# Score matmuls of even and odd heads by turns, value products one unit later, attention branch by rows first

## The chip, the core and the metric

The kernel runs on one NeuronCore of a Trainium2 chip. TensorE (PE in the rows) multiplies, ScalarE (ACT) and VectorE (DVE) do the elementwise work, GpSimd (POOL) a few powers, SyncE (SP) starts the DMAs. The metric is the time of one execution in microseconds of the device (us), less is better. Three runs of the kernel before gave 952.95, 954.09 and 954.66 us, median 954.09 us.

## What is computed

Two transformer blocks over one sequence of 256 tokens and 1024 features, float32. The first has a short convolution, a spatial gate, a mixture of 32 experts and a gated projection. The second, in which the change lies, is this, cut to what matters:

```
h = rmsnorm(x, norm_mix_pre)
conv_in, q, k, v, g_conv, g_att = split(h @ w_in)
u = silu(layernorm(causal_depthwise_conv(glu(conv_in), 31 taps)))
conv_out = u @ w_conv_branch + b_conv_branch
# stick-breaking attention, 8 heads of 64, queries in blocks of 128
z = einsum('bqhd,bkhd->bhqk', q, k) / 8
log_1m = where(s < t, log_sigmoid(-z), 0)
a = where(s < t, exp(log_sigmoid(z) + (reverse cumsum(log_1m) - log_1m)), 0)
att = einsum('bhqk,bkhd->bqhd', a, v)
att_out = att @ w_att_branch
merged = sigmoid(g_conv) * conv_out + sigmoid(g_att) * att_out
x = x + rmsnorm(merged @ w_out, norm_mix_post)
x = x + feed-forward(x)
```

## The kernel before

All 256 tokens are worked on at once, as two blocks `t` of 128. Weights stream from HBM in chunks of 1 MB, each cut into units of 128x1024 numbers. A unit is split by ACT (`whi`, L174 or L179) and DVE (`wlo`, L175 or L180) into a coarse and a fine part, and PE multiplies with both (`features`, L412; `tokens`, L423): 12 matmuls of 128x512 or 24 of 128x256 for a unit. Up to eight units are split ahead of the one in use; a split buffer comes free when PE is through with the unit that held it. After the experts four raw buffers of 1 MB hold the chunks in flight.

The order on every engine is the order in which the code is written; no scheduler changes it. `unit()` takes the next unit. In that call it lets the stream split ahead and run what was deferred (`ws.defer`), then does some taps of the depthwise convolution on DVE, and then the steps that the tables `ATT_AT`, `SIGMOIDS_AT` and `LN_AT` put at that unit's number. Only after that are the unit's own matmuls written. Units 4 to 15 give q, k and half of the convolution's input, 16 to 31 the two gates (four `n` of four units), 32 to 35 the attention branch.

The eight heads go in two groups `g`, four heads each, two even and two odd. A head's 64 features lie in one half of the 128 rows: even heads in rows 0 to 63, odd ones in 64 to 127. The steps of a group are: `att_z` (L1253, the scores, 12 float32 matmuls, each two records in the trace; then L1258, four bf16 matmuls for the mask), `att_exp` (L1263 to L1265), `att_log` (L1270), `att_add` (L1274, L1275), `att_sum` (L1279 to L1281), `att_a` (L1285, L1286) and `att_v` (L1296, L1297, the value products, whose result a deferred ACT copy L402 and a DVE subtraction L403 split into the coarse and fine `att`). The scores of even heads go to PSUM banks 4 and 5, those of odd heads to banks 6 and 7; `att_v` writes to the free halves of banks 5 and 7.

At units 32 to 34 the layer norm of the convolution stands among the branch: `ln_center` (L1365, the means, into bank 4; L1367 and L1368 centre and square; then `bias_parts`, L1342 to L1349), `ln_var` (L1374, sums of squares, into bank 5; L1377, a power on POOL, L1382) and `ln_out` (L1391 to L1397). `a_post` (L1408) multiplies the attention gate with the branch.

Of the kernel before, what the change touches and what calls it, by code (L numbers as in the profile page):

```python
# [46 lines left out]
OUT_AUTO = ()  # L47
CBN = 4
XT_AT = (5, 13)
ATT_AT = ((14, 14, 14, 14, 18, 18, 22), (25, 25, 26, 27, 30, 30, 31))  # L50
SIGMOIDS_AT = (28, 33)
LN_AT = (32, 33, 34)

# [169 lines left out]
def block_kernel(ctx: ExitStack, tc: tile.TileContext, x, pT, pk, rows, brow, wsT, bsp, w_1, w_gate,  # L223
                 w_up, w_down, w_ple_proj, w_2, out, dbg=None):
# [3 lines left out]
    nc = tc.nc  # L228
# [16 lines left out]
    def gain(name, k0):  # L245
        return lambda a: pc(name, k0 + a)

    gm4 = consts.tile([128, 8], F32, name="gm4")
    ws = Stream(nc, [(rawa, RAW_A), (rawb, RAW_B)], partp)
    ring = [RING]  # L250

    def add(src, a, b, cuts, gain=None, late=False, apart=False):
        pool, aside = 0, ASIDES.get(len(ws.chunks))
        if not late and not aside:
            pool = 0 if ring[0] % (RAW_A + RAW_B) < RAW_A else 1
            ring[0] += 1
        return ws.add(src, a, b, cuts, pool, gain, aside, apart)

    halves2 = [(0, 2, 0, 512), (2, 2, 0, 512)]
# [22 lines left out]
    def add_2(n, wide, gain=None):  # L282

        for _ in range(n):
            add(w_2[at_2[0]], 2 if wide else 4, 1024 if wide else 512, full2 if wide else halves2,
                gain and gain(at_2[0]), late=True)
            at_2[0] += 1

    at_2 = [0]
    add_2(4, True, lambda n: gain("g_ple", 2 * n))  # L290
    add_2(22, False)
    add_2(4, True)
    for j in range(13):
        if j < 11:
# [26 lines left out]
    def warm(ps, n):  # L321

        for _ in range(n):
            nc.tensor.matmul(ps[:, 0:128], ident_bf, ones_bf, start=True, stop=True, skip_group_check=True)  # L324
# [46 lines left out]
    def four(ap, n=4):  # L371
        return ap.rearrange("p (i t) -> p i t", i=n)
# [43 lines left out]
    def tokens(ps, hi, lo, u, k0, first, last, ts=(0, 1), cs=None):  # L416

        w = min(u.nb, 512)
        for k in range(u.na):
            for t in ts:  # L420
                for n, (a, b) in enumerate(((hi, u.hi), (hi, u.lo), (lo, u.hi))):
                    for c in cs or range(u.nb // w):
                        nc.tensor.matmul(ps[t][c], a[:, k0 + k, t, :], b[:, k, c * w:(c + 1) * w],  # L423
                                         start=(first and k == 0 and n == 0),
                                         stop=(last and k == u.na - 1 and n == 2), skip_group_check=True)
# [65 lines left out]
    with ExitStack() as pa:  # L491
# [90 lines left out]
        gu, csb, z = four(S3), four(S2), four(S1)  # L582
# [544 lines left out]
    def bank2(i):  # L1127
        return [bank(2 * i), bank(2 * i + 1)]
# [31 lines left out]
    def unit():  # L1160
        u = ws.get()
        conv_some(CONV_N[at_unit[0]] if at_unit[0] < len(CONV_N) else 0)
        for f in steps.get(at_unit[0], ()):
            f()
        at_unit[0] += 1
        return u
# [56 lines left out]
    qT = ab.tile([128, 4, 256], F32, name="qT")  # L1223
    kT = ab.tile([128, 4, 256], F32, name="kT")
# [16 lines left out]
    Z, EZ = {}, {}  # L1241

    def att_z(g):


        Z[g] = [bank2(2 + odd) for odd in range(2)]
        EZ[g] = [ab.tile([128, 768], F32, name=f"ez{odd}", bufs=2) for odd in range(2)]
        warm(Z[g][0][0], 0 if g else WARM4)
        for odd, (z, y) in enumerate(Z[g]):
            r = slice(odd * 64, odd * 64 + 64)  # L1250
            for o, ks, qs in ((z[:, 0:256], 0, 0), (z[:, 256:512], 0, 128), (y[:, 0:256], 128, 128)):
                for i in range(2):
                    nc.tensor.matmul(o[:, 128 * i:128 * i + 128], kT[r, 2 * g + i, ks:ks + 128],  # L1253
                                     qT[r, 2 * g + i, qs:qs + 128], start=(i == 0 and (ks, qs) != (0, 128)),
                                     stop=False, skip_group_check=True)
        for e, (z, y) in zip(EZ[g], Z[g]):
            for o in (z, y):
                nc.tensor.matmul(o[:, 0:256], ident_bf, cap[:, None, :].to_broadcast([128, 2, 128]),  # L1258
                                 start=False, stop=False, skip_group_check=True)
# [46 lines left out]

    for g, at in enumerate(ATT_AT):
        for n, f in zip(at, (att_z, att_exp, att_log, att_add, att_sum, att_a, att_v)):
            steps.setdefault(n, []).append(lambda f=f, g=g: f(g))
# [89 lines left out]
    for n, f in zip(LN_AT, (lambda: (ln_center(), bias_parts()), ln_var, ln_out)):  # L1399
        steps.setdefault(n, []).append(f)  # L1400

    for c in range(2):
        for i in range(2):
            tokens([[pa_[t][c]] for t in range(2)], ahv, alv, unit(), 2 * i, i == 0, i == 1)

        def a_post(c=c):
            for t in range(2):
                nc.vector.tensor_mul(G[t][:, 2 + c, :], G[t][:, 2 + c, :], pa_[t][c])  # L1408

        ws.defer(a_post)  # L1410
# [3 lines left out]
    for t in (1, 0):  # L1414
        for c in range(2):
            for f in range(4):
                nc.tensor.matmul(pc2[t][c][:, f * 128:f * 128 + 128],
                                 sel[:, 4 * c + f:4 * c + f + 1].to_broadcast([72, 128]), b3[2], start=(f == 0),
                                 stop=False, skip_group_check=True)
# [236 lines left out]
```

## Time and profile before

| | before |
|---|---|
| runs, us | 952.95, 954.09, 954.66 (median 954.09) |
| profiled execution, time | 954.75 us |
| profiled execution, span from first to last instruction | 953.1 us |
| mean granted TensorE clock | 0.955 of full speed |
| PE busy | 828.5 us (87%) |
| DVE busy | 395.6 us (42%) |
| ACT busy | 310.5 us (33%) |
| DMA | 288.98 MB, 303 GB/s on average |

The first 560 us hold the first block; there the experts' weights set the pace. From there to the end PE is busy nearly without a break, and ACT and DVE are busy beside it. The change lies between 635 and 730 us. Busy shares of the whole span say little on that stretch: what matters is which engine waits for which, place by place.

### The profile page before, as it was taken

Reading aid. Unit: us, or ns where it says so; the run is one execution under the profiler, and the core shown is the slowest. Engines: PE = TensorE matmul, PEld = TensorE weight load, DVE = VectorE, ACT = ScalarE, POOL = GpSimd, SP = SyncE. Lnnn points to the kernel's source line nnn. Section 1 sums busy time; section 2 is a strip of 40 time slices with the busy share of each in tenths; the row PEclk is TensorE's granted clock in tenths of the full one; section 3 lists DMA queues with packets and bytes.
Section 4 is the critical chain, followed back from the end, with each engine's and each line's share of the span. In section 5 each row is a group of like instructions: output and inputs, shape, how many; then the busy total and the mean of one; then the engine's idle time right before and its main releaser. Section 6 shows DMA issues by size and latency. Waiting matters only on the chain.

```text
span 953.1 us, 12639 instructions
## 1 busy us (share of the span) xinstructions
PE 828.5 (87%) x5187; PEld 543.6 (57%) x5187; DVE 395.6 (42%) x708; ACT 310.5 (33%) x488; POOL 12.8 (1%) x27
## 2 busy tenths in 40 slices
PE   8999987878677687676768789999999999999997
PEld 7998531313123131131222158997878889999995
DVE  5885410101001010010100077799888695565643
ACT  5643200000000000000000076768875574454531
POOL 0000000000000000000000000000000000000000
PEclk9999999988989898999879899999999999999999
DMA  9987899999999999999999984653434365555511
GB/s 312 419 328 308 328 420 421 420 420 420 421 420 421 420 421 420 421 419 422 420 416 421 419 346 177 230 178 122 156 134 137 129 231 206 196 185 177 182 41 44
DMA packets 42557, 288.98 MB, mean 303 GB/s; under 512 B 4968, under 2 KB 5632, under 8 KB 8832
## 3 DMA queue, kind: packets, MB, share of 16 engines
q1 hardware_dynamic: 42496, 288.13, 76.2%
q8 instruction: 42, 0.69, 0.3%
q14 instruction: 19, 0.16, 0.0%
HBM read 287.07 MB, written 1.05 MB: 302 GB/s over the span
## 4 chain that ended last, share of the span: by engine, by line
PE 52%; DMA 42%; DVE 2%; ACT 2%; issue 1%; POOL 0%; DVEq 0%; POOLq 0%; SPq 0%; ACTq 0%
PE bank L412 20%; PE bank L423 19%; DMA raw<-in_w_gate_dram 14%; DMA raw<-in_w_up_dram 13%; DMA raw<-in_w_down_dram 12%; PE pg L423 2%; DMA raw<-in_w_dram 2%; DMA gain<-in_pT_dram 2%; PE B L879 2%; PE pv L423 1%; PE A L879 1%; PE bank L739 1%; PE P L879 1%; PE bank L1253 1%; PE tp L324 0%
## 5 line engine op out<-in xcount | busy, mean ns | idle before, releaser
L412 PE MATMUL bank<-hi,whi 128*128 128x256 f32 x544 | 153.8, 283 | 0.0
L412 PE MATMUL bank<-lo,whi 128*128 128x256 f32 x544 | 153.0, 281 | 0.0
L412 PE MATMUL bank<-hi,wlo 128*128 128x256 f32 x544 | 152.9, 281 | 0.0
L879 PE MATMUL A<-raw,xg 128*32 128x512 f32 x512 | 100.2, 661 | 42.2 <-DMA raw<-in_w_gate_dram 42.2
L930 DVE SCALAR_TENSOR_TENSOR bsb<-B,sh,asb 128x512 f32<-128x512 f32 x8 | 6.0, 751 | 272.3 <-PE B L879 272.3
L879 PE MATMUL B<-raw,xg 128*32 128x512 f32 x480 | 91.3, 673 | 31.2 <-DMA raw<-in_w_up_dram 31.1
L175 DVE TENSOR_TENSOR wlo<-raw,whi 128x1024 fp32r<-128x1024 f32 x82 | 98.9, 1221 | 46.6 <-ACT whi L174 46.4
L180 DVE SCALAR_TENSOR_TENSOR wlo<-raw,pkt,whi 128x512 fp32r<-128x512 f32 (+1 forms) x136 | 98.5, 779 | 21.9 <-ACT whi L179 21.8
L179 ACT ACTIVATE whi<-raw,pkt 128x512 fp32r<-128x512 f32 (+1 forms) x136 | 92.3, 740 | 35.9 <-PE bank L412 16.4
L174 ACT CAST whi<-raw 128x1024 fp32r<-128x1024 f32 x82 | 84.5, 1047 | 59.7 <-PE bank L412 26.6
L412 PEld LDWEIGHTS bank<-lo,whi 128*128 128x128 f32 x544 | 102.6, 189 | 0.4
L412 PEld LDWEIGHTS bank<-hi,whi 128*128 128x128 f32 x544 | 102.3, 188 | 0.6 <-issue 0.2
L412 PEld LDWEIGHTS bank<-hi,wlo 128*128 128x128 f32 x544 | 102.6, 189 | 0.0
L879 PEld LDWEIGHTS A<-raw,xg 128*32 128x32 f32 x512 | 20.4, 116 | 113.3 <-DMA raw<-in_w_gate_dram 75.9
L879 PEld LDWEIGHTS B<-raw,xg 128*32 128x32 f32 x480 | 21.4, 121 | 96.9 <-DMA raw<-in_w_up_dram 60.6
L928 ACT ACTIVATE asb<-A,sh 128x512 f32<-128x512 f32 x8 | 5.5, 687 | 209.7 <-PE A L879 209.7
L879 PE MATMUL B<-raw,hs 128*32 128x512 f32 x256 | 49.2, 681 | 16.6 <-DMA raw<-in_w_down_dram 16.6
L423 PE MATMUL bank<-whi,hi 128*128 128x512 f32 x144 | 57.1, 410 | 1.3 <-ACT whi L179 1.3
L423 PE MATMUL bank<-wlo,hi 128*128 128x512 f32 x144 | 55.7, 401 | 0.3 <-DVE wlo L180 0.3
L423 PE MATMUL bank<-whi,lo 128*128 128x512 f32 x144 | 55.7, 400 | 0.0
L939 ACT COPY hs<-X 128x512 f32<-128x512 f32 x8 | 4.7, 585 | 151.2 <-PE X L937 151.2
L907 DVE COPY P<-B 128x512 f32<-128x512 f32 x8 | 5.5, 692 | 92.4 <-PE B L879 92.4
(315 smaller groups left out, 1058.1 us busy)
## 6 DMA issues: line engine op xcount, KB each, us to landing
raw<-in_w_dram SPq DMA_DIRECT2D x76, 1024.0 KB, 4.9
raw<-in_w_gate_dram SPq DMA_DIRECT2D x64, 1024.0 KB, 19.5
raw<-in_w_up_dram SPq DMA_DIRECT2D x60, 1024.0 KB, 19.8
raw<-in_w_down_dram SPq DMA_DIRECT2D x60, 1024.0 KB, 19.8
aside<-in_w_down_dram SPq DMA_DIRECT2D x8, 512.0 KB, 8.1
aside<-in_w_up_dram SPq DMA_DIRECT2D x2, 1024.0 KB
aside<-in_w_up_dram SPq DMA_DIRECT2D x4, 512.0 KB, 3.9
gain<-in_rows_dram SPq DMA_DIRECT2D x3, 512.0 KB, 6.5
```

Source lines behind the costliest of these rows:

```text
L174: nc.scalar.copy(u.hi, u.raw)
L175: nc.vector.tensor_tensor(u.lo, u.raw, u.hi.bitcast(F32), OP.subtract)
L179: nc.scalar.activation(u.hi[:, k], u.raw[:, k], AF.Identity, scale=g)
L180: nc.vector.scalar_tensor_tensor(u.lo[:, k], u.raw[:, k], g, u.hi[:, k].bitcast(F32), op0=OP.mult, op1=OP.subtract)
L412: nc.tensor.matmul(o, a[:, k, f * 128:(f + 1) * 128], b[:, k0 + k], start=(first and k == 0 and f % 2 == 0 and n == 0), stop=(last and k = ...
L423: nc.tensor.matmul(ps[t][c], a[:, k0 + k, t, :], b[:, k, c * w:(c + 1) * w], start=(first and k == 0 and n == 0), stop=(last and k == u.na ...
L739: nc.tensor.matmul(po[t][c][:, a % 512:a % 512 + b - a], l[:, i, t, :], r[:, 0, a:b], start=False, stop=(i == 3 and n == 2), skip_group_ch ...
L879: nc.tensor.matmul(ps[quarter(n)], lhs[:, quarter(n)], rows[n][k][:, w], start=first, stop=last, skip_group_check=True)
L907: nc.vector.tensor_copy(p, P[tag])
L928: nc.scalar.activation(sa, a, AF.Silu, scale=SH[q][:, 1:2])
L930: nc.vector.scalar_tensor_tensor(h, b, SH[q][:, 2:3], sa, op0=OP.mult, op1=OP.mult)
L1253: nc.tensor.matmul(o[:, 128 * i:128 * i + 128], kT[r, 2 * g + i, ks:ks + 128], qT[r, 2 * g + i, qs:qs + 128], start=(i == 0 and (ks, qs) ! ...
```

## The change

Three things are edited.

- In `att_z` the 12 score matmuls of a group alternate: one of an even head (rows 0 to 63), one of an odd head (rows 64 to 127). Before, the six of the even heads stood first, then the six of the odd ones. Operands, banks and number are the same.
- `att_v` of group 1 moves from unit 31 to unit 32. Its deferred split (L402 and L403) moves with it, from the call for unit 32 to the call for unit 33.
- The attention branch runs over its two halves of rows outside and over the two column halves `c` inside. So units 32 and 33 need group 0 alone and units 34 and 35 need group 1. The weights' units come in that order, a chunk's raw buffer is free one unit later for the first of the two chunks, and both `a_post` are deferred to the end.

```diff
-ATT_AT = ((14, 14, 14, 14, 18, 18, 22), (25, 25, 26, 27, 30, 30, 31))
+ATT_AT = ((14, 14, 14, 14, 18, 18, 22), (25, 25, 26, 27, 30, 30, 32))
...
-    add_2(22, False)
+    add_2(18, False)
+    for n in range(2):
+        cs = [add(w_2[at_2[0] + i], 4, 512, [] if n == 0 else halves2, late=True) for i in range(2)]
+        at_2[0] += 2
+        if n == 0:
+            for cut in halves2:
+                for c in cs:
+                    ws.unit(c, cut)
...
-        for odd, (z, y) in enumerate(Z[g]):
-            r = slice(odd * 64, odd * 64 + 64)
-            for o, ks, qs in ((z[:, 0:256], 0, 0), (z[:, 256:512], 0, 128), (y[:, 0:256], 128, 128)):
-                for i in range(2):
-                    nc.tensor.matmul(o[:, 128 * i:128 * i + 128], kT[r, 2 * g + i, ks:ks + 128],
-                                     qT[r, 2 * g + i, qs:qs + 128], start=(i == 0 and (ks, qs) != (0, 128)),
-                                     stop=False, skip_group_check=True)
+        for n, (ks, qs) in enumerate(((0, 0), (0, 128), (128, 128))):
+            for i in range(2):
+                for odd, (z, y) in enumerate(Z[g]):
+                    r = slice(odd * 64, odd * 64 + 64)
+                    o = (z, z[:, 256:512], y)[n][:, 128 * i:128 * i + 128]
+                    nc.tensor.matmul(o, kT[r, 2 * g + i, ks:ks + 128], qT[r, 2 * g + i, qs:qs + 128],
+                                     start=(i == 0 and n != 1), stop=False, skip_group_check=True)
...
+    for i in range(2):
+        for c in range(2):
+            tokens([[pa_[t][c]] for t in range(2)], ahv, alv, unit(), 2 * i, i == 0, i == 1)
+
     for c in range(2):
-        for i in range(2):
-            tokens([[pa_[t][c]] for t in range(2)], ahv, alv, unit(), 2 * i, i == 0, i == 1)
-
         def a_post(c=c):
```

Two places where instructions move bear on what follows. In the changed file lines stand 7 or 8 further down (L1381 is L1374 of before).

The first is PE at the end of unit 32: the last matmuls of that unit's branch (L423; `att` is the split attention), then the first of `ln_var`. In square brackets stand the engines whose semaphores an instruction waits for. Before:

```order
L423 MATMUL bank<-wlo,att 128x512
L423 MATMUL bank<-whi,att 128x512
L1374 MATMUL bank<-nones,conv 128x1 [waits PE_49,Activation_49]
L1374 MATMUL bank<-nones,conv 128x1 [waits Activation_49]
L1374 MATMUL bank<-nones,sg 128x1 [waits Activation_49] x2
```

And now:

```order
L430 MATMUL bank<-wlo,att 128x512
L430 MATMUL bank<-whi,att 128x512
L1381 MATMUL bank<-nones,conv 128x1 [waits DVE_49,PE_49]
L1381 MATMUL bank<-nones,conv 128x1 [waits Activation_49]
L1381 MATMUL bank<-nones,sg 128x1 [waits Activation_49] x2
```

The first matmul of `ln_var` now waits for DVE. It writes to bank 5, whose other half holds the value products of group 1; the DVE instruction that it waits for is the first of the two subtractions that read them (L410, L403 before).

The second is DVE around `ln_center`: two splits of weights (`wlo`), the centring of `conv`, the parts of the bias, the next split. Before:

```order
L175 TENSOR_TENSOR wlo<-raw,whi 128x1024 x2
L403 TENSOR_TENSOR att<-bank,att 128x256 x2
L1367 SCALAR_TENSOR_TENSOR conv<-bank,conv 128x256 x4
L1343 TENSOR_TENSOR bias<-bias,b_4665 72x128
L1345 TENSOR_TENSOR bias<-bias,b_4666 72x128
L1346 TENSOR_TENSOR bsel<-ident 72x8
L1347 TENSOR_TENSOR sel<-bsel,ident 72x8
L175 TENSOR_TENSOR wlo<-raw,whi 128x1024
L1377 TENSOR_SCALAR q<-bank 128x2
```

And now:

```order
L175 TENSOR_TENSOR wlo<-raw,whi 128x1024 x2
L1374 SCALAR_TENSOR_TENSOR conv<-bank,conv 128x256 x4
L1350 TENSOR_TENSOR bias<-bias,b_4657 72x128
L1352 TENSOR_TENSOR bias<-bias,b_4658 72x128
L1353 TENSOR_TENSOR bsel<-ident 72x8
L1354 TENSOR_TENSOR sel<-bsel,ident 72x8
L175 TENSOR_TENSOR wlo<-raw,whi 128x1024
L410 TENSOR_TENSOR att<-bank,att 128x256 x2
L1384 TENSOR_SCALAR q<-bank 128x2
```

The two subtractions of the value products stood ahead of the centring; they now stand behind it, behind the parts of the bias and behind one more split of weights. On ACT the two copies that feed them move in the same way, from ahead of the squares (L1368) to behind the same unit's `whi`.

## Rows read from the trace of the kernel before

**Rows 1.** Chain that ended last, 635 to 700 us: start, us, engine, line.

```profile
635.73 2.53 PE bank L1253 x24
...
677.66 0.60 ACT ez L1263
...
699.40 0.65 PE bank L1296 x2
```

**Rows 2.** Busy time by engine in three stretches (us and instructions), clock granted.

```profile
650.00:677.00 27.00, 27.00 (x135) 21.10 (x134) 26.88 (x49) 20.50 (x34) 0.00 (x0) 1.00 0.47 162
685.80:708.80 23.00, 21.81 (x115) 16.84 (x114) 22.82 (x43) 18.88 (x31) 0.00 (x0) 1.00 0.36 126
715.00:946.40 231.40, 231.40 (x1454) 207.24 (x1453) 144.15 (x212) 116.46 (x179) 2.75 (x5) 1.00 0.44 154
```

**Rows 3.** Timeline of PE, pieces of 0.4 us: records in hand in each.

```profile
635.66 0.93 PE L1253 MATMUL bank<-qT,kT 64*128 64x128 f32 x6
...
636.66 0.93 PE L1253 MATMUL bank<-qT,kT 64*128 64x128 f32 x9
```

**Rows 4.** Timeline of PE at the first value products, 664.5 to 664.8 us.

```profile
664.71 0.44 PE L1296 MATMUL bank<-ez,vt 128*64 128x256 f32 x2
```

**Rows 5.** Waits, 635 to 650 us: total, times, longest.

```profile
ACT ez L1263 <- PE bank L1258: 2.4, 1, 2.4
...
DVE ez L1274 <- ACT ez L1270: 1.9, 1, 1.9
```

**Rows 6.** Waits of DVE, 677 to 690 us, and of PE, 633 to 760 us.

```profile
DVE wlo L175 <- ACT whi L174: 2.5, 2, 2.0
...
PE bank L1296 <- ACT ez L1286: 1.2, 1, 1.2
```

**Rows 7.** Timeline of ACT, 675 to 712 us.

```profile
675.91 1.70 ACT L1191 ACTIVATE tap<-upad,pkt 128x256 f32<-128x256 f32 x4
...
710.97 1.05 ACT L174 CAST whi<-raw 128x1024 fp32r<-128x1024 f32 x1
```

**Rows 8.** Timeline of DVE, 701 to 714 us.

```profile
701.30 3.26 DVE L1201 SCALAR_TENSOR_TENSOR conv<-upad,pkt,conv 128x256 f32<-128x256 f32 x8
704.47 2.36 DVE L175 TENSOR_TENSOR wlo<-raw,whi 128x1024 fp32r<-128x1024 f32 x2
706.74 0.75 DVE L403 TENSOR_TENSOR att<-bank,att 128x256 fp32r<-128x256 f32 x2
707.41 1.41 DVE L1367 SCALAR_TENSOR_TENSOR conv<-bank,conv 128x256 f32<-128x256 f32 x4
...
712.05 1.23 DVE L175 TENSOR_TENSOR wlo<-raw,whi 128x1024 fp32r<-128x1024 f32 x1 [1.35 <-ACT whi L174]
```

**Rows 9.** Timeline of PE, 706 to 710.5 us.

```profile
706.22 1.08 PE L1365 MATMUL bank<-conv,nones 128*128 128x256 f32 x4
709.93 0.50 PE L1374 MATMUL bank<-nones,conv 128*128 128x1 f32 x4
```

**Rows 10.** Timeline of PE near the start: a gap, then matmuls at two paces.

```profile
9.09 0.51 PE L423 MATMUL bank<-whi,hi 128*128 128x512 f32 x1 [1.29 <-ACT whi L179]
...
11.51 0.63 PE L423 MATMUL bank<-whi,hi 128*128 128x512 f32 x1
11.93 0.63 PE L423 MATMUL bank<-wlo,hi 128*128 128x512 f32 x1
...
14.58 0.39 PE L423 MATMUL bank<-whi,lo 128*128 128x512 f32 x1
14.81 0.40 PE L423 MATMUL bank<-whi,hi 128*128 128x512 f32 x1
```

**Rows 11.** Stretches as in Rows 2, with the granted clock third from the end.

```profile
10.80:14.10 3.30, 3.30 (x10) 2.56 (x9) 3.24 (x9) 2.81 (x7) 1.10 (x1) 0.50 1.02 428
...
699.40:703.00 3.60, 3.60 (x23) 2.81 (x24) 3.53 (x8) 1.64 (x3) 0.00 (x0) 1.00 0.53 175
...
949.50:952.90 3.40, 0.00 (x0) 0.00 (x0) 0.57 (x1) 0.00 (x0) 0.00 (x0) 0.50 0.40 154
```

## The prediction

> **What bounds the kernel now.** I read the chain of waits first, then the busy time by stretches, then the timelines of the three engines between 635 and 715 us. The chain shows two score groups of 2.53 us each on PE, and between the second and 699.4 us it leaves PE: it goes through ACT (677.66 us) and DVE and comes back to PE at the second group's value products [rows 1]. That is the only place after the experts where PE stands still: 1.2 us, for the exponentials of ACT [rows 6]. From 715 us on PE is busy in every one of 231.4 us [rows 2]. So whatever PE loses or gains up to 715 us goes one to one into the end. ACT and DVE are nearly as full: DVE has 26.88 of 27.0 us between 650 and 677 us and 22.82 of 23.0 from 685.8 to 708.8 us [rows 2]. In that second stretch DVE has no slack that an earlier PE could use, which is the reader's key to what follows.
>
> **Scores by turns.** A group's 24 records take 2.53 us [rows 1], 0.105 us each. In a piece of 0.4 us within the even half 6 records are in hand; in one at the turn from even to odd, 9 [rows 3]. So the two row halves do run side by side when both are next in the queue. The odd half begins at 636.66 us, 1.00 us after the even one, and takes the remaining 1.53 us by itself. With the halves by turns I expect both to take about 1.5 us together: −1.0 us a group. The bounds are 0 (no overlap) and −1.27 (half of 2.53). The nearest precedent is the value products, where the two column halves begin within 0.01 us of each other: two records in 0.44 us [rows 4]; I take the value nearest to it.
>
> Two rules of the Trainium skill bear on this. TensorEngine Tiling (Array Packing), Restrictions and Gotchas, says that different row tiles cannot use the same PSUM bank at once; here even scores go to banks 4 and 5 and odd ones to 6 and 7, so it would not take the gain away. TensorE: Matmul & The Clock Gate, Part 3: Packing small matmuls, reports 3.07 times for four row tiles, 77% of the ideal; by an estimate from it two tiles would give 1.54 times, a saving of 0.9 instead of 1.0 us a group.
>
> Where do the two savings go? After group 0, ACT had waited 2.4 us for that very group, and DVE 1.9 us for ACT [rows 5], so ACT and DVE both move 1.0 us ahead, and DVE carries this through its full stretch. Group 1 helps PE alone: ACT reaches that group's exponentials at 677.66 us, right behind its own taps, which end at 675.91 + 1.70 = 677.61 us [rows 1, 7]. DVE's one pause after that, 2.5 us, is for ACT [rows 6]. So in the second stretch DVE is 1.0 us earlier, not 2.0.
>
> **Value products one unit later.** The 1.2 us that PE waited [rows 6] go: 12 more matmuls stand before the products. But their split moves too. On DVE it moves from ahead of the centring to behind the centring, the bias parts and one more `wlo`; on ACT from ahead of the squares to behind that unit's `whi`. And PE's first `ln_var` matmul, which writes into the same bank, now waits for it. Behind that matmul on PE stands everything else: units 33 to 35, both branches, the rest of the kernel. I work out when it is released.
>
> Before, the centring starts at 707.41 us, after the two subtractions at 706.74 us [rows 8]. Without these it starts 0.67 us earlier, and with the 1.0 us of above at 705.74 us. The means that it needs are there: the convolution's last taps end at 704.56 − 1.0 = 703.56 us, and the last two mean products with what follows them take 1.08 us [rows 8, 9].
> Then the chain of before holds: from the centring at 707.41 us over squares and bias parts to `whi` on ACT (710.97 + 1.05 = 712.02 us [rows 7]), then `wlo` on DVE (712.05 + 1.23 = 713.28 us [rows 8]), 5.87 us in all. Behind it the first subtraction takes about 0.4 us (0.75 for two [rows 8]) and can overlap its predecessor a little: 6.25 us. So `ln_var` starts at 705.74 + 6.25 = 712.0 us. Before it started at 709.93 us [rows 9]. That is **+2.0 us**, with both savings and the lost wait already in it. PE, for its part, is at that point at 703.6 + 1.0 + 2.8 (12 matmuls of 0.23 us [rows 10]) = 707.4 us, so it **stands idle for some 4.5 us**. Bounds: +1.7 with scores at −1.27, +2.9 if DVE moves by nothing.
>
> **The clock.** Near the start PE waited 1.29 us for its first weights, and from 10.8 us on the granted clock was 0.50, the 1.2 GHz level; the matmuls then came 0.42 us apart, at full clock 0.23 [rows 10, 11]. After PE's last matmul the clock was at 0.50 too (949.5 us) [rows 11]. After the 1.2 us of before it stayed at 1.00 (699.4 us) [rows 11]. An idle time of 4.5 us, followed by `ln_var`'s products of one column [rows 9], is longer than any of those between matmuls, so I expect a fall. One low stretch as at the start, 3.3 us at about half pace, costs 1.6 us where it lies on matmuls wholly, less where it lies on the idle time, and twice that if a second follows: 0 to 3.3 us, and I take **1.5 us**.
>
> The page TensorE: Matmul & The Clock Gate, Why this matters for your kernels, warns against idle gaps between bursts of matmuls, since they put the clock back to half; its sum would be the same 1.5 us, and it makes the fall likelier than rows of such unequal gaps do.
>
> **Branch by rows first.** It issues the same 48 matmuls. Its first two units need group 0 alone, so the late split does not hold them; the next two come after `ln_var` anyway. The raw buffer that comes free a unit later costs nothing while PE, from 715 us on, never waits [rows 2]; if that cover failed, one DMA late would show as a wait of `whi`. The first `a_post` pair now follows behind: 1.3 us more on DVE before the merges, against a PE that is itself over 2 us later. I put it at 0, with a bound of +1.
>
> **Sum.** 954.75 (profiled execution) + 2.0 + 1.5 = 958.25 us. The median of the runs, 954.09, lies 0.66 us lower; against it the change gives 957.6 us, and this I predict.
>
> **Rivals.**
> *It gains what it saves* (faster). Mechanism: the split of the value products is done before PE comes to `ln_var`, so 2.0 us of scores and 1.2 us of wait go and nothing takes their place: 954.09 − 3.2 = 950.9 us. For it: both savings are real in the rows. Against: PE arrives at 707.4 us, and the subtraction would have to end 4.6 us sooner than its chain allows; it stands behind instructions that themselves need the means. It decides from the point where the split ends before about 707.4 us. 0.07.
> *The clock stays up.* Only the wait is left: 954.09 + 2.0 = 956.1 us. For it: after 1.2 us the clock held. 0.15, half of it within 0.2%.
> *The halves don't overlap* (the change doesn't do what it says). Then DVE keeps its time and `ln_var` starts at 713.0 us: +2.9, with the clock +4.4, 958.5 us. Against: 9 records in hand at the turn [rows 3]. 0.06.
> *Group 1 helps DVE as well.* If ACT's taps at 675.91 us also come earlier than by 1.0 us, because they hang on PE and not on ACT's own work, DVE is up to 2.0 us ahead and `ln_var` starts at 711.0 us: +1.0, with the clock +2.5, so 955.1 or 956.6 us. Against: the exponentials follow the taps with 0.05 us between them [rows 1, 7]. 0.10, half with a fall of the clock.
>
> **How the numbers follow.** My forecast has 0.62. 0.2% (1.9 us) is about what a measurement of this kernel can tell from no change, so the limits are 952.2 and 956.0 us. Slower: the forecast but for a small part (0.60), half of the clock's rival (0.07), the missing overlap (0.06), half of the last (0.05): 0.78. Same: 0.02 + 0.08 + 0.05 = 0.15. Faster: 0.07. The range goes at its high end to 954.09 + 2.0 + 3.3 = 959.4 us, the clock at its dearest; at its low end it takes in +1.0 without a fall, 955.1 us, less half a microsecond by which runs differ: 954.6 us.
>
> **What would show it.** The 12 score matmuls of a group in about 1.5 us. No wait at the value products. One wait of PE of 4 to 5 us for DVE at `ln_var`, its releaser the attention's subtraction; a granted clock of 0.50 for some us behind it; `ln_var` about 2 us later than before, and the end by as much and by what the clock takes. I am wrong if PE reaches `ln_var` after the split, if the centring starts much before 705.7 us, or if the clock holds.

## The result and the profile after

| | before | after |
|---|---|---|
| runs, median of 6 each, us | 954.35 (952.95 to 954.72) | 960.19 (959.20 to 961.22) |
| ratio of after to before, 95% interval | | 1.0064 [1.0051, 1.0077] |
| profiled execution, us | 954.75 | 960.03 |
| its span, us | 953.1 | 958.4 |
| PE, DVE, ACT busy, us | 828.5, 395.6, 310.5 | 827.2, 395.6, 310.4 |
| mean granted clock | 0.955 | 0.952 |

The change makes the kernel slower by 0.64%, 5.8 us on the medians. DVE and ACT have no more to do. PE's 1.3 us less come from the first block, where it was busy for 440.9 instead of 443.8 us up to 560 us; behind that it is busy 1.6 us longer, though the scores take 2.0 us less. The time is lost in waiting and in a lower clock, between 706 and 720 us. The forecast was 957.6 us, slower, with 959.4 us as the upper end: the sign is right, the size too small by 2.6 us and outside the range.

First what went as forecast. PE's timeline of after has both score groups, 24 records each (columns as in [rows 3]: start, us, what):

```profile
635.11 1.61 PE L1261 MATMUL bank<-qT,kT 64*128 64x128 f32 x24
...
673.26 1.61 PE L1261 MATMUL bank<-qT,kT 64*128 64x128 f32 x24
```

The row of before for the same 24 records is this:

```profile
635.66 2.60 PE L1253 MATMUL bank<-qT,kT 64*128 64x128 f32 x24
```

Each group is 0.99 us shorter. In the chain of waits of after the first group has this row, against 2.53 us in [rows 1]:

```profile
635.18 1.54 PE bank L1261 x24
```

Second, the waits of PE from 600 us to the end, in after (total, times, longest); in before the only one was the 1.2 us at the value products [rows 6]:

```profile
PE bank L1381 <- DVE att L410: 4.9, 1, 4.9
PE bank L1286 <- DVE ez L1281: 0.5, 1, 0.5
```

The wait at the value products is gone, and the forecast one stands at the variance, for the subtraction that splits the value products. The chain of waits of after leads up to it (start, us, engine and line):

```profile
705.03 0.43 DVE conv L1374
...
708.72 1.05 ACT whi L174
...
709.79 1.23 DVE wlo L175
711.02 0.35 DVE att L410
711.37 0.14 issue
711.50 3.55 PE bank L1381 x16
715.05 4.96 PE bank L430 x12
```

And the same place in before:

```profile
710.09 1.68 PE bank L1374 x16
711.77 2.91 PE bank L423 x12
```

Centring, squares and bias parts, `whi`, `wlo`, subtraction: the chain that the prediction followed by hand. PE stands still from 706.64 us (its last product, 706.25 + 0.39) to 711.50 us. The two last rows are where the forecast fell short: the same 16 records of the variance (8 products of one column, two records each) and 12 matmuls of the branch take 8.51 us instead of 4.59. Counted in the timelines from the first product to the next instruction they take 8.35 instead of 4.59 us, 3.8 us more; the chain of before sets in 0.16 us late. The stretches of after say why (columns as in [rows 2], the granted clock third from the end):

```profile
706.70:709.20 2.50, 0.00 (x0) 0.00 (x0) 0.82 (x4) 2.06 (x7) 0.00 (x0) 1.00 0.89 360
709.20:711.50 2.30, 0.00 (x0) 0.03 (x1) 1.71 (x3) 2.28 (x4) 0.00 (x0) 0.50 0.06 25
711.50:715.00 3.50, 3.50 (x17) 3.50 (x17) 0.19 (x1) 1.26 (x3) 0.00 (x0) 0.50 0.00 0
715.00:719.40 4.40, 4.40 (x12) 3.43 (x12) 0.64 (x3) 0.00 (x0) 0.69 (x1) 0.50 0.00 0
719.40:725.00 5.60, 5.60 (x28) 4.59 (x27) 3.25 (x7) 4.55 (x7) 0.00 (x0) 1.00 0.29 80
```

The clock falls to 0.50 (1.2 GHz) in the middle of the idle time and stays there for 10.2 us, all through the one-column products of the variance and for another 4.4 us of matmuls of 512 columns.

**A finer measure.** Runs of one kernel lie up to 3.3 us apart. In the profiled executions part of that is plain: the score groups begin between 634.0 and 635.8 us, whatever the kernel: what stands ahead of them takes a little more or less. So the table of experiments has, beside the medians, the length of the changed part within the profiled execution: from the first record of the first score group to the end of PE's last matmul. Before it is 946.04 + 0.39 − 635.66 = 310.77 us, after 951.34 + 0.39 − 635.11 = 316.62 us, so +5.85 us. It rests on one trace of each kernel, so a difference of a tenth of a us decides nothing by itself. The rows for the two ends are

```profile
946.04 0.39 PE L423 MATMUL bank<-whi,flo 128*128 128x512 f32 x1
```

for before and, for after,

```profile
951.34 0.39 PE L430 MATMUL bank<-whi,flo 128*128 128x512 f32 x1
```

### The profile page after: what moved, and what is told of

Its sections match the earlier page's. It is cut to its first block, busy times and chain, and to the rows that moved or that the text cites. A ratio compares the mean times of both kernels' runs of the same rounds, so it can differ in the third digit from the quotient of the medians.

```text
span 958.4 us, 12638 instructions
## 1 busy us (share of the span) xinstructions
PE 827.2 (86%) x5187; PEld 544.2 (57%) x5187; DVE 395.6 (41%) x708; ACT 310.4 (32%) x488; POOL 12.7 (1%) x27
## 4 chain that ended last, share of the span: by engine, by line
PE 50%; DMA 43%; DVE 4%; ACT 2%; issue 1%; POOL 0%; DVEq 0%; POOLq 0%; SPq 0%; ACTq 0%
PE bank L419 20%; PE bank L430 18%; DMA raw<-in_w_down_dram 14%; DMA raw<-in_w_gate_dram 14%; DMA raw<-in_w_up_dram 12%; PE pg L430 2%; DMA raw<-in_w_dram 2%; DMA gain<-in_pT_dram 2%; PE pv L430 1%; PE A L886 1%; PE P L886 1%; DVE conv L1208 1%; DVE wlo L175 1%; PE bank L746 1%; PE B L886 1%
## 5 line engine op out<-in xcount | busy, mean ns | idle before, releaser
L886 PE MATMUL B<-raw,xg 128*32 128x512 f32 x480 | 88.8, 656 | 34.2 <-DMA raw<-in_w_up_dram 34.1
L886 PE MATMUL B<-raw,hs 128*32 128x512 f32 x256 | 51.7, 708 | 18.5 <-DMA raw<-in_w_down_dram 18.5
```

The lines of the kernel that those rows point to most:

```text
L886: nc.tensor.matmul(ps[quarter(n)], lhs[:, quarter(n)], rows[n][k][:, w], start=first, stop=last, skip_group_check=True)
```

## The experiments

Twelve kernels ran, in three groups of four; each group had its own runs of before beside it.

| run | what it is | median, us | before beside it | ratio, 95% interval | changed part, us against before |
|---|---|---|---|---|---|
| after | all three edits | 960.19 | 954.35 | 1.0064 [1.0051, 1.0077] | +5.85 |
| e1_scores | before, scores by turns alone | 953.58 | 953.76 | 0.9997 [0.9988, 1.0006] | −1.18 |
| e2_no_turns | after without scores by turns | 961.47 | 953.76 | 1.0086 [1.0072, 1.0100] | +6.48 |
| e3_warm | after, 64 extra matmuls in the gap | 958.51 | 953.76 | 1.0051 [1.0037, 1.0064] | +5.29 |
| e9_warm_full | after, 84 of them | 956.62 | 954.45 | 1.0028 [1.0018, 1.0038] | +2.18 |
| e12_dense_first | after, 60 of them behind the gap | 961.37 | 954.42 | 1.0068 [1.0053, 1.0084] | +7.71 |
| e4_bank | after, variance in bank 4 | 953.46 | 953.76 | 0.9996 [0.9987, 1.0005] | −1.01 |
| e5_at_once | after, split at once | 953.47 | 954.45 | 0.9993 [0.9985, 1.0002] | −0.84 |
| e6_not_moved | after, value products at unit 31 | 953.33 | 954.45 | 0.9987 [0.9978, 0.9996] | −1.11 |
| e7_bias_later | e5_at_once, bias parts later | 953.45 | 954.42 | 0.9986 [0.9977, 0.9995] | −0.89 |
| e8_not_moved_bias | e6_not_moved, bias parts later | 952.94 | 954.42 | 0.9983 [0.9974, 0.9992] | −1.19 |
| e10_bank_bias | e4_bank, bias parts later | 951.69 | 954.45 | 0.9971 [0.9960, 0.9982] | −2.75 |
| e11_bank_no_turns | e10_bank_bias, scores as before | 952.98 | 954.42 | 0.9984 [0.9975, 0.9993] | −1.58 |

### The two halves of the change, apart

*Scores by turns alone.* The edit is the second hunk of the diff, put into the kernel before.

> The kernel before with one edit of the three: scores of even and odd heads by turns. Theory: a group takes 1.5 us instead of 2.5, but only the first group's saving gets through ACT and DVE to the second group's value products, so PE waits there for ACT some 2.2 us instead of 1.2 and the end moves by 1.0 us: 953.3 us against 954.3, no wait at the variance, granted clock 1.00 from 690 to 720 us. Rival 'both savings reach the end': 952.3 us and still 1.2 us of wait. Rival 'what PE gains early is lost elsewhere': 954.3 us.

The changed part is 1.18 us shorter. The medians show only 0.2 us, with an interval of −1.1 to +0.6 us that holds 1.0 us but not the 2.0 us of the first rival. It holds zero too, so it is the trace alone that speaks against the second rival. PE's waits show where the rest went:

```profile
PE bank L1296 <- ACT ez L1286: 1.2, 1, 1.2
PE bank L1279 <- DVE ez L1274: 0.5, 1, 0.5
```

The saving of the second group turns into waiting, but not where I put it: the wait at the value products stays 1.2 us, and a new one of 0.5 us stands a step earlier, in that group's sums, for DVE.

*The rest alone.*

```diff
-        for n, (ks, qs) in enumerate(((0, 0), (0, 128), (128, 128))):
-            for i in range(2):
-                for odd, (z, y) in enumerate(Z[g]):
...
+        for odd, (z, y) in enumerate(Z[g]):
...
+            for o, ks, qs in ((z[:, 0:256], 0, 0), (z[:, 256:512], 0, 128), (y[:, 0:256], 128, 128)):
+                for i in range(2):
```

> The changed kernel with the scores as before (even heads first, then odd), so the value products one unit later and the branch by rows first are alone. Theory: DVE loses the 1.0 us that the first score group gave it, the variance's first matmul starts 3 us later than before instead of 2.1, and the low clock behind it costs about 4 us as in the changed kernel: 954.3 + 3.1 + 4.0 = 961.3 us. Rival 'the clock costs 1.5 us and something unseen the rest': the same stall, but the granted clock low for about 3 us and the end not later than 959 us. Rival 'the scores by turns gain nothing for the end': 960.2 us as the changed kernel.

961.47 us, and the wait is there as in after (the first row is of PE's waits, the others of its timeline):

```profile
PE bank L1381 <- DVE att L410: 4.8, 1, 4.8
712.65 0.90 PE L1381 MATMUL bank<-nones,conv 128*128 128x1 f32 x4 [4.80 <-DVE att L410]
...
715.97 0.77 PE L430 MATMUL bank<-whi,att 128*128 128x512 f32 x1
```

PE goes on 3.28 us later than in before (712.65 − 635.10 against [rows 9]'s 709.93 − 635.66), 1.16 us later than in after. The forecast bound of "DVE moves by nothing" was +2.9 us; by the prediction's own numbers it should have been 706.74 + 6.25 − 709.93 = +3.06 us. The clock falls only at the end of the gap:

```profile
707.70:712.60 4.90, 0.15 (x1) 0.00 (x0) 2.48 (x7) 4.44 (x11) 0.00 (x0) 1.00 0.52 206
712.70:716.00 3.30, 3.30 (x17) 3.30 (x17) 0.13 (x1) 1.20 (x3) 0.00 (x0) 0.51 0.00 0
716.00:719.50 3.50, 3.50 (x9) 2.76 (x10) 0.64 (x3) 0.00 (x0) 0.69 (x1) 0.50 0.00 0
```

It is low for 6.8 us here, not 10.2, though the gap and the products behind it are the same; all of it lies on work. It costs 6.48 − 3.28 = 3.2 us.

### What the clock costs

*64 extra matmuls in the gap.*

```diff
     def ln_var():
         var = LN["d"][1]
+        warm(LN["w"], 64)
```

(`warm` is the helper at L331 that issues bf16 matmuls of 128x128; `LN["w"]` is the bank that takes the extra matmuls beside the means; a line there, not shown, gives it this name.)

> The changed kernel with 64 extra bf16 matmuls of 128x128 (about 3.7 us by the rows of such matmuls elsewhere in the program) into a bank that is free, written on PE just ahead of the variance; they add work and no result. The wait for the second subtraction of the value products stays, but PE is at work in most of it. Theory 'stall 2.1 us, low clock 4 us': the clock stays at 1.00 at the variance, its 16 records take about 1.7 us instead of 3.55, the next 12 matmuls 2.8 instead of 4.96, and the time is 954.3 + 2.1 = 956.4 us. Rival 'the 4 us come from something else behind the variance (the order of the branch, late weights)': the time stays at 960 us though the clock is up. Rival 'the clock falls all the same, for lack of work in the variance itself': 958 to 960 us with the granted clock at 0.50 behind it.

The first theory fell. The time is 958.5 us, and the clock fell all the same, 1.3 us after the variance had begun; so the forecast of the second rival stood, for this dose. The wait left over is 1.25 us (the first two rows; the last two are stretches with the granted clock):

```profile
711.91 0.58 PE L1383 MATMUL bank<-nones,conv 128*128 128x1 f32 x4 [1.25 <-DVE att L410]
...
714.15 0.77 PE L430 MATMUL bank<-whi,att 128*128 128x512 f32 x1
711.90:713.10 1.20, 1.19 (x11) 1.20 (x12) 0.19 (x1) 1.19 (x3) 0.00 (x0) 1.00 0.00 0
713.20:720.00 6.80, 6.80 (x21) 5.64 (x21) 0.64 (x3) 0.34 (x1) 0.69 (x1) 0.50 0.01 2
```

The matmuls of 512 columns set in at 714.15 us, and the clock stayed at 0.50 for another 5.8 us. The low stretch cost 5.29 − 2.11 = 3.2 us (the variance starts 711.91 − 635.53 = 76.38 us behind the scores, 2.11 us later than in before). The question left was whether the remaining gap or the variance's own products brought the clock down.

*84 of them*, in the same place, which closes the gap.

> As the run with 64 extra bf16 matmuls ahead of the variance, with 84 of them (about 4.9 us), which fills the whole wait for the split: PE has no gap over 0.3 us there. They add work and no result. With 64 the clock still fell, 1.3 us after the variance had begun, behind a gap of 1.25 us. Theory 'a gap ahead of the variance's one-column products brings the clock down': no fall, granted clock 1.00 from 700 to 725 us, and the time is the stall alone, 953.8 + 2.1 = 955.9 us. Rival 'the variance's own products bring it down once small matmuls stand ahead of them': a fall to 0.50 at 713 us as with 64, and 958.5 us again.

The clock holds, as the first theory said:

```profile
707.18 4.86 PE L331 MATMUL bank<-ones_bf,ident_bf 128*128 128x128 bf16 x84
712.18 0.58 PE L1383 MATMUL bank<-nones,conv 128*128 128x1 f32 x4
...
713.96 0.48 PE L430 MATMUL bank<-whi,att 128*128 128x512 f32 x1
```

The stretches around it:

```profile
712.20:714.00 1.80, 1.80 (x17) 1.80 (x17) 0.17 (x1) 1.24 (x3) 0.00 (x0) 1.00 0.04 9
714.00:720.00 6.00, 6.00 (x29) 4.94 (x30) 2.51 (x7) 2.61 (x3) 0.69 (x1) 1.00 0.00 0
```

Everything of after is still there, the late split too (the variance starts 712.18 − 635.79 = 76.39 us behind the scores, in after 711.50 − 635.11 = 76.39 us); and the clock is up. The time is 2.2 us above before. So of the 5.8 us the stall is 2.2 and the clock 3.7 us (5.85 − 2.18). This is the run that splits the loss.

*60 of them behind the gap*, in the variance's own bank, so that they wait as its products did.

```diff
         var = LN["d"][1]
+        warm(var, 60)
```

> The changed kernel with 60 extra bf16 matmuls of 128x128 written into the variance's own bank, ahead of its products, so that they wait for the split as these did: the gap of 4.9 us stays, but behind it PE first has about 3.5 us of dense work (at full clock) and only then the products of one column. They add work and no result. In the changed kernel the clock came back 7.9 us after the gap's end, 4.5 us after matmuls of 512 columns had set in. Theory 'the one-column products don't bring the clock back, dense work does': 0.50 from before the gap's end to some 3.5 to 6 us behind it, so back by 717.5 us, and the loss of clock moves to the extra matmuls: 953.8 + 2.1 + 3.5 + 2 to 3 = 961.4 to 962.4 us. Rival 'the low stretch has its length from the gap': 0.50 for 10 us, until about 719.5 us, the variance at 3.5 us, and 953.8 + 2.1 + 3.5 + 4.0 = 963.4 us.

The gap is the same, 4.75 us, and the clock falls in it as in after. But now it is back 4.9 us behind the gap's end, not 7.9 (the first two rows are PE's timeline):

```profile
711.71 5.82 PE L331 MATMUL bank<-ones_bf,ident_bf 128*128 128x128 bf16 x60 [4.75 <-DVE att L410]
717.37 0.56 PE L1382 MATMUL bank<-nones,conv 128*128 128x1 f32 x4
709.80:711.70 1.90, 0.00 (x0) 0.00 (x0) 1.61 (x3) 1.88 (x4) 0.00 (x0) 0.50 0.00 0
711.70:716.50 4.80, 4.79 (x46) 4.79 (x47) 0.28 (x1) 1.36 (x3) 0.00 (x0) 0.50 0.00 0
716.70:725.00 8.30, 8.30 (x58) 7.28 (x56) 2.35 (x6) 2.45 (x3) 0.69 (x1) 1.00 0.01 2
```

The 60 matmuls take 717.37 − 711.71 = 5.66 us; at the pace of the run with 84 (712.18 − 707.18 = 5.00 us) they would take 3.57. So the clock costs 2.1 us here against 3.7 in after, and 2.0 (stall) + 3.6 (added work) + 2.1 = 7.7 us is the measured +7.71. The rival, a low stretch of 10 us whatever follows the gap, is refuted. The theory is not shown by that: the whole low stretch is 6.8 us here with dense work first and 6.8 us in e2_no_turns with the one-column products first, and in e3_warm 5.8 us of matmuls of 512 columns ran before the clock was back.

What the runs do agree on is the price. Low clock on work, and what it cost: 7.9 us and 3.7 us in after, 6.8 and 3.2 in e2_no_turns, 6.8 and 3.2 in e3_warm, 4.9 and 2.1 here. That is 0.43 to 0.47 us for each us in which PE worked at 0.50.

### What makes PE wait

*The variance's sums in bank 4.*

```diff
-        var = LN["d"][1]
+        var = LN["d"][0][:, 256:258]
```

> The changed kernel with the variance's sums written to the free half of bank 4 instead of bank 5, so that its first matmul no longer shares a bank with the second group's value products and needs no subtraction of DVE first. Order on all engines as in the changed kernel. Theory: PE comes to the variance at about 707 us and goes on; no wait of 4.9 us, granted clock 1.00, the first score group's 1.0 us is left: 953.3 us (a wait of 1 to 2 us at the layer norm's output for the power may show, since DVE reaches it late). Rival 'the wait is for DVE's squares or the split of weights anyway, not for the bank': PE stands still 3 to 5 us at the variance all the same and the time is 957 us or more.

The wait at the variance is gone, and with it the low clock; the power's input is late instead, by the 1.5 us that were expected:

```profile
PE bank L1398 <- DVE diag L1389: 1.5, 1, 1.5
PE bank L1286 <- DVE ez L1281: 0.5, 1, 0.5
```

The stretches have the clock at 1.00 on both sides of that wait and in it:

```profile
705.00:710.00 5.00, 5.00 (x30) 4.16 (x30) 2.45 (x10) 3.89 (x11) 0.00 (x0) 1.00 0.61 211
710.00:715.00 5.00, 3.50 (x17) 2.62 (x16) 3.49 (x7) 4.95 (x7) 0.69 (x1) 1.00 0.00 0
```

So without the shared bank there is no stall at the variance, with the same order on all engines. The changed part is 1.01 us shorter than before.

*The split at once.*

```diff
-            ws.defer(lambda i=i, pt=pt: split(ahi[:, 2 * g + i], alo[:, 2 * g + i], pt))
+            f = lambda i=i, pt=pt: split(ahi[:, 2 * g + i], alo[:, 2 * g + i], pt)
+            f() if g else ws.defer(f)
```

> The changed kernel with one thing undone: the split of the second group's value products is no longer deferred to the next unit's call but written right behind the products, ahead of the squares on ACT and of the bias parts and the next split of weights on DVE. Value products one unit later, scores by turns and the branch by rows first stay, and the variance still shares their bank. Theory 'it is the place of the split in DVE's and ACT's queues': PE waits at the variance under 1 us or not at all, the granted clock stays at 1.00, and the first score group's 1.0 to 1.2 us remain: 952.7 us against 953.8 (1 us of wait at the layer norm's output, for the power, may show). Rival 'value products so late make PE wait in any case': 3 us of wait or more at the variance and 957 us or more.

953.5 us and no wait at the variance: the stall needs both, the shared bank and the split's late place in the queues. But the clock was not at 1.00. With no gap of PE the trace has this:

```profile
706.50:708.60 2.10, 2.10 (x17) 2.00 (x17) 1.07 (x5) 1.72 (x7) 0.00 (x0) 1.00 0.88 367
708.60:709.50 0.90, 0.90 (x6) 0.77 (x6) 0.23 (x2) 0.85 (x3) 0.00 (x0) 1.00 0.49 200
709.60:712.90 3.30, 3.30 (x9) 2.54 (x8) 1.78 (x4) 3.02 (x4) 0.69 (x1) 0.50 0.00 0
```

The variance took 708.62 − 706.49 = 2.13 us here, its first products a little apart (ACT's squares of the second half end at 707.44 us, 0.28 us after the products of that half set in), against 713.96 − 712.18 = 1.78 us above. About a microsecond of ordinary matmuls later the clock was low for 3.4 us; that cost the 12 matmuls behind it 1.5 us (713.05 − 708.62 = 4.43 us against 716.85 − 713.96 = 2.89).

*The value products back at unit 31.*

```diff
-ATT_AT = ((14, 14, 14, 14, 18, 18, 22), (25, 25, 26, 27, 30, 30, 32))
+ATT_AT = ((14, 14, 14, 14, 18, 18, 22), (25, 25, 26, 27, 30, 30, 31))
```

> The changed kernel with the second group's value products back at unit 31: scores by turns and the branch by rows first alone. Theory: PE waits for ACT at the value products, 1.2 to 1.7 us, as before the change, none at the variance, clock 1.00, and the branch's order costs nothing: as scores by turns alone, 952.7 us (1.0 to 1.2 us under the kernel before). Rival 'the branch by rows first costs something by itself': 954 us or more, with a wait of PE or a gap behind 710 us that the scores alone did not have.

The changed part is −1.11 us here and −1.18 us with scores by turns alone, and the intervals of the medians overlap: no cost of the branch by rows first shows. The wait at the value products is back, none is at the variance, and the clock is at 1.00:

```profile
PE bank L1303 <- ACT ez L1293: 1.2, 1, 1.2
```

### A version that beats both

What stands between the variance and the layer norm's output on DVE are the bias parts, one split of weights and the split of the value products. The bias parts can wait:

```diff
-    for n, f in zip(LN_AT, (lambda: (ln_center(), bias_parts()), ln_var, ln_out)):
+    for n, f in zip(LN_AT, (ln_center, lambda: (ln_var(), bias_parts()), ln_out)):
```

With the variance in bank 4:

> The run with the variance's sums in bank 4 (no sharing with the value products), and the parts of the bias, which stood on DVE and ACT ahead of the next split of weights, written one unit later, behind the variance. In the former run PE waited 1.5 us at the layer norm's output for the power's input, which DVE reached behind bias parts, a split of weights and the split of the value products. Theory: these come up to 2 us earlier, that wait goes wholly or nearly, and the time is 953.8 - 1.0 - 1.5 = 951.3 us. Rival 'the bias parts are missed later, where the convolution's branch needs them': the wait of 1.5 us goes and one for the bias or a split of weights takes its place before 730 us, 952.5 to 953.5 us.

951.69 us against 954.45, ratio 0.9971 [0.9960, 0.9982]: 2.8 us faster than before, and some 8.5 us less than after. PE's waits from 600 us on are down to one:

```profile
PE bank L1286 <- DVE ez L1281: 0.5, 1, 0.5
```

Three more runs ask which parts of it are needed.

*The split at once and the bias parts later*, the variance still in bank 5:

> The run with the split of the value products at once, and the parts of the bias written one unit later, behind the variance, as in the best run so far. In the former run the trace showed no wait of PE over 0.3 us at the variance, but a granted clock of 0.50 from 709.6 to 713.0 us, with the variance's first two groups of products at 0.57 to 0.67 us each instead of 0.45. Theory 'the squares on ACT stand behind the split's copies, so the variance trickles and the clock falls whatever the bias does': low clock for about 3.4 us again and 953 us (before: 954). Rival 'that fall was of that one run': clock 1.00 throughout and 951.5 us, as with the variance in bank 4.

The clock fell again, in the same place and for as long, with the variance at 2.13 us once more (706.99 to 709.12 us):

```profile
707.00:709.10 2.10, 2.10 (x17) 2.00 (x17) 0.68 (x3) 2.08 (x5) 0.00 (x0) 1.00 0.85 351
709.90:713.30 3.40, 3.40 (x9) 2.63 (x8) 1.59 (x8) 2.69 (x8) 0.69 (x1) 0.50 0.00 0
```

The changed part is 1.86 us longer than in e10_bank_bias; 1.5 us of it is the clock and 0.35 the thin products themselves.

*The value products not moved, the bias parts later:*

> Scores by turns, the branch by rows first and the bias parts one unit later, with the second group's value products back at unit 31. Asks whether the move of the value products is worth having once nothing waits for their split. Theory: PE waits 1.2 us for ACT at the value products and 0.5 us in the second group's sums, so 1.0 to 1.2 us of the scores are left and the bias parts give nothing: 953 us against 954.2, some 1.5 us more than the best run. Rival 'the bias parts were the gain': 951.6 us.

The changed part is −1.19 us, the wait of 1.2 us is there: the bias parts give nothing by themselves. The move of the value products, together with the variance in bank 4, is worth 1.6 us (−2.75 against −1.19).

*Scores as before in the best version:*

> The best run so far (variance in bank 4, bias parts one unit later, value products one unit later, branch by rows first) with the scores as before, even heads first. Asks what the scores by turns are worth once PE's two waits are gone. Theory: PE loses 2.0 us of scores, and the wait of 0.5 us in the second group's sums goes, so the whole is the 1.2 us of wait at the value products alone: 953.0 us against 954.2, 1.5 us above the best run. Rival 'the scores gain nothing for the end': 951.6 us.

−1.58 us in the changed part, −1.4 on the medians, and PE has no wait left: without the turns the move, with bank 4 and the later bias parts, brings a little more than its 1.2 us, and the scores by turns add 1.2 of their 2.0 us.

## Why the prediction was right in sign and wrong in size

**Scores by turns: right.** −1.0 us a group was forecast, −0.99 measured. The estimate from the Trainium skill's page TensorE: Matmul & The Clock Gate, Part 3: Packing small matmuls, was a saving of 0.9 us; the trace gives a factor of 2.53 [rows 1] to 1.54, 1.64 times, a little more than the 1.54 of that estimate. So the rival "the halves don't overlap" fell. That the second group's saving does not move DVE was right too, though [rows 6] has two waits of DVE for ACT, 2.5 us together, and not one pause: with both groups by turns the variance starts 1.16 us earlier than without, little more than one group's 0.99. So "Group 1 helps DVE as well" fell as well.

**The new wait: right.** Forecast: released by the attention's subtraction, PE idle some 4.5 us, the variance 2.0 us later. Measured: that releaser, 4.85 us, and 76.39 − (709.93 − 635.66) = 2.12 us. The run with the variance in another bank shows the cause, not only the releaser: without the shared bank the same order on all engines has no stall. Its upper bound was added up wrongly, +2.9 for +3.06 us (e2_no_turns: +3.28).

**The branch by rows first at 0: right**, as far as the runs can tell (0.07 us between the single traces of e1_scores and e6_not_moved).

**The clock at +1.5 us: this step failed.** That the clock would fall was right, and so was the price: 1.6 us for 3.3 us on matmuls is 0.48 us for each, and the runs have 0.43 to 0.47. Wrong was how long it would be low while PE works: "one low stretch as at the start, 3.3 us", two at most, part of it on the idle time. Measured were 10.2 us at 0.50, of which 2.3 lay on the idle time and 7.9 on work; the loss is 3.7 us, above the bound of 3.3. The variance's records lie in it too and take twice as long, 3.55 us in the chain instead of 1.68. The start of the kernel was no measure for this place: there a wait of 1.29 us stands ahead and matmuls of 512 columns follow [rows 10], here a wait of 4.85 us stands ahead and products of one column follow. Which of these differences makes the stretch longer is not shown. With 3.7 instead of 1.5 us the sum would have been 954.09 + 2.0 + 3.7 = 959.8 us, 0.4 us from the result.

The Trainium skill's page TensorE: Matmul & The Clock Gate, Why this matters for your kernels, warns of idle gaps. Its rule agrees with the trace where the gap was 4.75 to 4.85 us (after, e2_no_turns, e12_dense_first). It does not cover e5_at_once and e7_bias_later, where the clock fell with PE never idle.

**The rivals.** "The clock stays up", 956.1 us, is what e9_warm_full measured when the clock was made to stay up, 956.6 us. So the sign did not hang on the clock. "It gains what it saves", 950.9 us, was not the result, but its mechanism is real: in e10_bank_bias, with nothing in the way of PE at the variance, the gain is 2.75 us of the 3.2. The rest is about the 0.5 us of the new wait in the second group's sums, which no row of before showed. The point from which I let it decide, a split that ends before 707.4 us, was one way of two; the shorter one is that the variance need not wait for the split at all.

**What stays open.** What sets the length of a low stretch is not settled: after and e2_no_turns have the same wait and the same products behind it, and 10.2 against 6.8 us. In after the clock fell in the middle of the wait, in e2_no_turns at its end. Nor is it settled why the clock fell in e5_at_once and e7_bias_later, where PE never stood idle and the variance took 0.35 us longer, while a wait of PE of 1.5 us left it at 1.00 in e4_bank. Each of these lengths is from one trace. How far the loss varies from run to run is not either: the five runs of e3_warm lie between 956.7 and 959.9 us, wider than those of after, and only the slowest of them, 959.89 us, has a trace.

## What to carry to other kernels

Before a step is moved on one engine, look at what shares its PSUM bank: in this program a matmul into the free half of a bank waited for the readers of the other half, and these stood far back in another engine's queue. When PE is about to stand still for some microseconds, put a price on the clock too, and allow for a low stretch much longer than one seen behind a shorter gap: here waits of 4.75 to 4.85 us moved PE's work by 2.0 to 3.3 us, and the low clock behind them cost another 2.1 to 3.7 us. A saving on the bounding engine that ends in front of a wait for another one is worth only what the other one can be moved by. And a wait that is there only because two results share a bank can be taken away by one changed line (e4_bank).

## What the runs showed of the hardware

- In three runs with a gap of PE of 4.75 to 4.85 us the clock fell to 0.50 within the gap or at its end and stayed there for 10.2 us (after), 6.8 us (e2_no_turns) and 6.8 us (e12_dense_first). Behind the gap PE ran the variance's 8 products of one column and then matmuls of 512 columns in the first two, bf16 matmuls of 128 columns in the third. With a gap of 1.25 us ahead of the same products the clock fell in the midst of them, for 6.8 us (e3_warm); 84 bf16 matmuls in place of the gap kept it at 1.00 (e9_warm_full).
- Each us of work at 0.50 cost 0.43 to 0.47 us (after, e2_no_turns, e3_warm, e12_dense_first).
- Two kernels without any gap of PE fell to 0.50 for 3.4 us, about a microsecond after the variance's products, which took 2.13 us in them (e5_at_once, e7_bias_later). Where they took 1.7 to 1.8 us with no gap ahead, in before, e9_warm_full and e10_bank_bias, the clock held.
- Two float32 matmuls on 64 rows each, in different halves of the rows and by turns in the queue, give 1.64 times the pace of one half after the other (24 records in 1.54 instead of 2.53 us).
